# A gated short-convolution block: the input projection in triples of column groups, 20 block products each, in place of pairs with 7

## The chip, the cores and the metric

The kernel runs on one core of one Trainium2 chip. The metric is the device time of one execution in microseconds (us); lower is better. The engines are named as in the profile: PE (TensorE, the matmuls), PEld (its weight loads), DVE (VectorE), ACT (ScalarE), POOL (GpSimd) and SP (SyncE, which here only issues DMA transfers).

## The reference, cut to what matters

With DEPTH = 1 only the first kind of layer is computed. x is 1024 tokens by 1024 features, `w_in` is 1024 by 8192 and `w_out` 2048 by 1024, all in float32.

```python
def rms_norm(x, g):
    y = xf * lax.rsqrt(jnp.mean(xf * xf, axis=-1, keepdims=True) + EPS)
    return y * g

def short_conv_mixer(u, w_in, conv_w, w_out):
    z, bg, cg, v = jnp.split(u @ w_in.astype(u.dtype), 4, axis=-1)
    y = bg * causal_dwconv(cg * v, conv_w) * jax.nn.silu(z)
    return y @ w_out.astype(u.dtype)

h = h + rms_norm(short_conv_mixer(rms_norm(h, pre_norm), ...), post_norm)
```

The convolution has three taps over the tokens and works on each of the 2048 channels by itself. The four parts Z, BG, CG and V of the projection are 2048 columns each.

## The kernel before, in words

**Tiling.** The channels are cut into 16 chunks of 128. A group is one chunk of one part: 128 columns of `w_in`, so there are 64 groups. The projection's result stands transposed: the 128 channels of a group on the partitions, the tokens in two halves of 512, each in a PSUM bank (`bank`). Every operand of a product is split into a high and a low part in float32r, and every product of two blocks is three matmuls (low by high, high by low, high by high, L189 to L191), each with a 128x128 weight block and 512 tokens.

**Pairs and their 7 products.** `PAIRS` has 32 pairs of groups, (CG, V) and then (Z, BG) of each chunk. Pair 0 is multiplied plainly (`plain`, L384 to L386, 96 matmuls). Each of the other 31 is a 2x2 by 2x2 block product (two groups by two halves of the inner dimension, against two halves of the inner dimension by two halves of the tokens) done with 7 block products in place of 8; `ORDER` is "abcedfg". A block product has four 128-wide parts of the inner dimension and three matmuls each, so a pair has 84. Seven operand forms of the tokens (`u_a` to `u_g`, high and low) are built once, in the head, and stay in SBUF: `new_u`, L352 and L355 for those read straight from the transposed tokens in PSUM, L489, L531, L532, L545 and L547 for the others.

**What the other engines do for a pair.** POOL forms the four sums of weight blocks, each 128x512 (`add_s`, L133 to L137). `split_w` splits the weights in four parts: ACT makes the high part (L140), DVE the low part (L141). PSUM is read by ACT (`snap`, L197) and DVE (`after`, L213 to L236). POOL multiplies the gates (L220, L226, L228). When a chunk's CG and V are there, `conv` runs the three taps, one on ACT (L583) and two on DVE (L585), over all 1024 tokens. `y_done` stores the chunk's y to DRAM.

**The operands of the output projection.** The output projection is one 2x2 by 2x2 block product in 7 as well. Sums of blocks of y and of `w_out` are made in DRAM during the projection by accumulating DMAs on POOL's queue (`more`, L241; `add_y`, `fetch_t`, `add_t`). Then 28 units of 1 MB are fetched (`fetch_unit`), split (`split_unit`), and multiplied (`out_mm`, L718 to L720, 672 matmuls), with the post norm between and behind.

**What sets the order.** `tc.manual_schedule()`: each engine works through its instructions in the order in which the program issues them. An instruction that waits holds up all that stand behind it on its engine. So the order of the calls in the loop over pairs (products, `after`, `split_w` of the next pair, `add_s` of the next pair) is the order on every engine.

**The head.** Tokens are loaded, their norm is folded into the transposes on PE (L340), and the first token half is read out as operand forms a and b. Pair 0's products for that half and the first products of pair 1 (b, a) stand on PE between the transposes of the second token half and the building of the forms c to g.

Of the kernel before, what the change touches and what calls it, by code (L numbers as in the profile page):

```python
# [8 lines left out]
F32 = mybir.dt.float32  # L9
# [9 lines left out]
def kernel(  # L19
# [26 lines left out]
    KH = NK // 2  # L46
    TH = NT // 2
# [10 lines left out]
    up = ctx.enter_context(tc.tile_pool(name="up", bufs=7))  # L58
    wp = ctx.enter_context(tc.tile_pool(name="wp", bufs=3))
    raw = ctx.enter_context(tc.tile_pool(name="raw", bufs=3))  # L60
# [21 lines left out]

# [27 lines left out]
    PAIRS = [(c, tys) for c in range(NC) for tys in ((CG, V), (Z, BG))]  # L110
    raws, sums, wt = {}, {}, {}

    def fetch(p, rows=(0, 1)):
        if p >= len(PAIRS):
            return
        c, tys = PAIRS[p]
        if p not in raws:
            raws[p] = raw.tile([P, 2, NK, P], F32, tag="raw", name=f"raw_{p}")
        for n in rows:
            c0 = tys[n] * CI + c * P  # L120
            nc.sync.dma_start(raws[p][:, n], wiv[:, :, c0 : c0 + P])

    def add_s(p, part):

        if p >= len(PAIRS):
            return
        r = raws[p]
        a11, a12, a21, a22 = (flat(r[:, n, k * KH : (k + 1) * KH]) for n in (0, 1) for k in (0, 1))
        if part == 0:
            sums[p] = raw.tile([P, 4, HB], F32, tag="sum", name=f"sum_{p}", bufs=1)  # L130
        s = sums[p]
        if part == 0:
            nc.gpsimd.tensor_add(s[:, 1], a21, a22)  # L133
            nc.gpsimd.tensor_sub(s[:, 0], s[:, 1], a11)  # L134
        else:
            nc.gpsimd.tensor_sub(s[:, 2], a11, a21)  # L136
            nc.gpsimd.tensor_sub(s[:, 3], a12, s[:, 0])  # L137
# [5 lines left out]
    def split_w(p, part):  # L143

        if p >= len(PAIRS):
            return
        n = 2 * HB if part < 3 else HB
        tag = "w8" if part < 3 else "w4"
        if p == 1 and part == 1:
            t = raw.tile([P, 2, n], F32R, tag="raw", name=f"w{part}_{p}")  # L150
        else:
            t = wp.tile([P, 2, n], F32R, tag=tag, name=f"w{part}_{p}", bufs=3 if part < 3 else 2)
        if part == 0:
            src = flat(raws[p][:, 0])
        elif part == 3:
            src = flat(raws[p][:, 1, KH:])
        else:
            src = flat(sums[p][:, 2 * (part - 1) : 2 * part])
        split(src, t[:, 0], t[:, 1])
        wt[p, part] = t  # L160


    WHERE = {"a": (0, 0), "b": (0, HB), "c": (1, 0), "e": (1, HB), "d": (2, 0), "f": (2, HB), "g": (3, 0)}
    ORDER = "abcedfg"
    UH, UL = {}, {}

    def new_u(i):
        u = up.tile([P, 2, KH, HB], F32R, tag="u", name=f"u_{i}")
        UH[i], UL[i] = u[:, 0], u[:, 1]

    for i in ORDER[:-1]:
        new_u(i)

    banks = {}

    def product(p, i, ks=None):

        part, off = WHERE[i]
        w = wt[p, part]
        which = {"b": "y", "e": "v", "f": "v"}.get(i, "x")  # L180
        first = i in "abe"
        if first and (p, which) not in banks:
            banks[p, which] = bank(f"p{which}_{p}")
        ps = banks[p, which]
        for k in range(KH) if ks is None else ks:
# [9 lines left out]
    def snap(p, i):  # L195
        t = snp.tile([P, HB], F32, tag="sn", name=f"sn{i}_{p}", bufs=5)
        nc.scalar.copy(t, banks[p, "v" if i == "e" else "x"])  # L197
        sn[p, i] = t
# [5 lines left out]
    def after(p, i):  # L204
# [4 lines left out]
        if i in "ace":  # L209
            snap(p, i)  # L210
# [629 lines left out]
```

## Time and profile before

| what | value |
|---|---|
| median of 2 runs | 796.25 us (795.71 to 796.79) |
| the profiled execution, its own time | 797.52 us |
| the profiled execution, span in the trace | 795.7 us |
| PE busy, matmuls and transposes | 784.0 us, 3502 |
| DVE, POOL, ACT busy | 472.7, 337.0, 307.3 us |
| bytes moved by DMA | 116.49 MB |
| first matmul of pair 0 | 13.23 us |
| first matmul of the output projection | 636.53 us |
| last matmul | 788.63 us |

The profile is one execution; its time is 1.8 us longer than its span and 1.27 us over the median. The trace gives each instruction's start and length in us from the span's start. A matmul's own length is modelled, so the pace of PE is read from the distance between starts. A row of the grouped view names the line, engine, operation, output and inputs, the number of instructions, their busy time and mean length in ns, and then the idle time of the engine just ahead of them with what ended it. Some matmul records are missing from the trace.

### The profile page before, as it was taken

Reading aid. Unit: us, or ns where it says so; the run is one execution under the profiler, and the core shown is the slowest. Engines: PE = TensorE matmul, PEld = TensorE weight load, DVE = VectorE, ACT = ScalarE, POOL = GpSimd, SP = SyncE. Lnnn points to the kernel's source line nnn. Section 1 sums busy time; section 2 is a strip of 40 time slices with the busy share of each in tenths; the row PEclk is TensorE's granted clock in tenths of the full one; section 3 lists DMA queues with packets and bytes.
Section 4 is the critical chain, followed back from the end, with each engine's and each line's share of the span. In section 5 each row is a group of like instructions: output and inputs, shape, how many; then the busy total and the mean of one; then the engine's idle time right before and its main releaser. Section 6 shows DMA issues by size and latency. Waiting matters only on the chain.

```text
span 795.7 us, 9148 instructions
## 1 busy us (share of the span) xinstructions
PE 784.0 (99%) x3502; PEld 648.5 (82%) x3502; DVE 472.7 (59%) x518; ACT 307.3 (39%) x425; POOL 337.0 (42%) x256
## 2 busy tenths in 40 slices
PE   8999999999999999999999999999999999999996
PEld 8877888888888887888788888888888888888885
DVE  6799646554645454654466565656565856633766
ACT  7555333232333333333333343323233646544441
POOL 1608646465454555547664545455445110000020
PEclk9999999999999999999999999999999999999999
DMA  9131373829191928295633425161606589455237
GB/s 317 55 106 40 81 210 68 224 54 253 25 264 38 241 66 212 75 257 114 137 96 90 126 60 145 40 170 16 173 14 180 217 278 348 176 202 212 105 112 259
DMA packets 100811, 116.49 MB, mean 146 GB/s; under 512 B 4328, under 2 KB 69920, under 8 KB 98720
## 3 DMA queue, kind: packets, MB, share of 16 engines
q1 hardware_dynamic: 91536, 99.13, 37.6%
q0 software_dynamic: 9216, 16.78, 13.8%
q8 instruction: 27, 0.44, 0.2%
q14 instruction: 16, 0.13, 0.0%
q10 hardware_dynamic: 16, 0.00, 0.0%
HBM read 92.83 MB, written 44.04 MB: 172 GB/s over the span
## 4 chain that ended last, share of the span: by engine, by line
PE 90%; issue 4%; POOL 3%; DVE 1%; ACT 1%; DMA 0%; DVEq 0%; POOLq 0%; ACTq 0%
PE px L189 13%; PE px L191 13%; PE px L190 13%; PE pv L191 7%; PE pv L189 7%; PE pv L190 7%; PE po_x L718 4%; PE po_x L719 4%; PE po_x L720 4%; PE py L191 3%; PE py L189 3%; PE py L190 3%; PE po_v L718 2%; PE po_v L720 2%; PE po_v L719 2%
## 5 line engine op out<-in xcount | busy, mean ns | idle before, releaser
L141 DVE TENSOR_TENSOR w<-sum,w 128x1024 fp32r<-128x1024 f32 x62 | 88.2, 1422 | 120.3 <-ACT w L140 120.3
L141 DVE TENSOR_TENSOR w<-raw,w 128x1024 fp32r<-128x1024 f32 (+1 forms) x62 | 94.3, 1522 | 5.9 <-ACT w L140 5.9
L140 ACT CAST w<-sum 128x1024 fp32r<-128x1024 f32 x62 | 64.9, 1047 | 65.8 <-issue 54.5
L585 DVE SCALAR_TENSOR_TENSOR cv<-gpad,cw,cv 128x1024 f32<-128x1024 f32 x32 | 55.6, 1739 | 33.1 <-ACT cv L583 32.5
L140 ACT CAST w<-raw 128x1024 fp32r<-128x1024 f32 (+1 forms) x62 | 51.4, 831 | 50.0 <-PE py L191 41.4
L758 POOL TENSOR_TENSOR acc<-xr,acc 128x512 f32<-128x512 f32 x4 | 6.9, 1734 | 117.6 <-DVE acc L757 117.6
L136 POOL TENSOR_TENSOR sum<-raw 128x512 f32<-128x512 f32 x31 | 55.7, 1798 | 0.0
L134 POOL TENSOR_TENSOR sum<-sum,raw 128x512 f32<-128x512 f32 x31 | 54.0, 1743 | 2.4
L223 DVE TENSOR_TENSOR snc<-pv,snc 128x512 f32<-128x512 f32 x30 | 20.7, 690 | 54.8 <-PE pv L191 54.8
L220 POOL TENSOR_TENSOR sne<-sne,cv 128x512 f32<-128x512 f32 x15 | 20.8, 1387 | 70.7 <-DVE sne L218 70.7
L137 POOL TENSOR_TENSOR sum<-raw,sum 128x512 f32<-128x512 f32 x31 | 50.7, 1637 | 0.0
L133 POOL TENSOR_TENSOR sum<-raw 128x512 f32<-128x512 f32 x31 | 47.4, 1529 | 7.0 <-DVE w L141 7.0
L189 PE MATMUL px<-u_g,w 128*128 128x512 f32 x124 | 48.5, 391 | 1.4 <-DVE sne L218 0.8
L189 PE MATMUL px<-u_c,w 128*128 128x512 f32 x124 | 48.5, 391 | 1.3 <-ACT sna L197 1.3
L189 PE MATMUL px<-u_d,w 128*128 128x512 f32 x124 | 48.4, 390 | 0.2 <-ACT snc L197 0.2
L189 PE MATMUL py<-u_b,w 128*128 128x512 f32 x124 | 48.5, 391 | 0.0
L189 PE MATMUL px<-u_a,w 128*128 128x512 f32 x124 | 48.3, 390 | 0.0
L190 PE MATMUL px<-u_c,w 128*128 128x512 f32 x124 | 48.3, 389 | 0.0
L190 PE MATMUL px<-u_g,w 128*128 128x512 f32 x124 | 48.3, 389 | 0.0
L191 PE MATMUL px<-u_g,w 128*128 128x512 f32 x124 | 48.3, 389 | 0.0
L191 PE MATMUL px<-u_d,w 128*128 128x512 f32 x124 | 48.3, 389 | 0.0
L191 PE MATMUL py<-u_b,w 128*128 128x512 f32 x124 | 48.3, 389 | 0.0
(248 smaller groups left out, 2051.2 us busy)
## 6 DMA issues: line engine op xcount, KB each, us to landing
raw<-in_sc_w_in SPq DMA_DIRECT2D x64, 512.0 KB, 7.7
s_d<-cv SPq DMA_DIRECT2D x32, 256.0 KB, 2.2
t_d<-in_sc_w_out SPq DMA_DIRECT2D x32, 256.0 KB, 5.9
s_d<-cv POOLq DMA_DIRECT2D x16, 256.0 KB, 6.1
t_d<-in_sc_w_out POOLq DMA_DIRECT2D x16, 256.0 KB, 7.3
t_d<-t_d POOLq DMA_DIRECT2D x16, 256.0 KB, 4.3
y_d<-cv SPq DMA_DIRECT2D x8, 512.0 KB, 3.8
s_d<-s_d POOLq DMA_DIRECT2D x16, 256.0 KB, 6.1
```

Of the source, the lines that this page charges most:

```text
L134: nc.gpsimd.tensor_sub(s[:, 0], s[:, 1], a11)
L136: nc.gpsimd.tensor_sub(s[:, 2], a11, a21)
L137: nc.gpsimd.tensor_sub(s[:, 3], a12, s[:, 0])
L140: nc.scalar.copy(hi, src)
L141: nc.vector.tensor_sub(lo, src, hi.bitcast(F32))
L189: nc.tensor.matmul(ps, lo, UH[i][:, k], start=first and k == 0, stop=False, skip_group_check=True)
L190: nc.tensor.matmul(ps, hi, UL[i][:, k], start=False, stop=False, skip_group_check=True)
L191: nc.tensor.matmul(ps, hi, UH[i][:, k], start=False, stop=last, skip_group_check=True)
L585: nc.vector.scalar_tensor_tensor(cv, gpad[:, j : j + L], tap(c, j), cv, op0=ALU.mult, op1=ALU.add)
L718: nc.tensor.matmul(ps, lo, u[:, 0, k], start=first, stop=False, skip_group_check=True)
L719: nc.tensor.matmul(ps, hi, u[:, 1, k], start=False, stop=False, skip_group_check=True)
L720: nc.tensor.matmul(ps, hi, u[:, 0, k], start=False, stop=last, skip_group_check=True)
```

## The change

**Triples and 20 products.** The 64 groups stand in one list in the order CG, V, Z, BG of each chunk. The first four are multiplied plainly (192 matmuls). The other 60 are 20 triples. A triple is three groups by four quarters of the inner dimension, against four quarters by two token halves: 24 block products, done as 20. Each block product has two 128-wide parts and three matmuls each, so a triple has 120 matmuls. A triple no longer falls on a chunk's border: since a chunk has four groups, the parts in the triple's columns 1, 2, 0 (`COL`) run (CG, V, Z), (BG, CG, V), (Z, BG, CG), (V, Z, BG) and then start again. The text below and the prediction call these four kinds P0, P1, P2 and P3.

**Operand forms.** 18 forms of the tokens, each a high and a low part of 2x512 columns, are kept (`up`, 18 buffers). Eight are the blocks b00 to b31 themselves, read from PSUM. For the others the head adds and subtracts blocks (`make`, on DVE or POOL, L585, L587, L589) and splits the result (`finish`: ACT L126, DVE L127). The forms u_17, 6, 4, 11, 16, 10, 2 and 19 are finished behind the first splits of triple 0.

**Weights.** `sums` forms the weight sums of the next triple in place and in `e` (17 adds of 128x256 and one of 128x512 on POOL, L176 to L191). `split_w` splits units of two products' weights, A to J, into four buffers; six of the ten units are two pieces of 128x256.

**PSUM.** The 20 products run through five chains (`CHAINS`), each in one bank. Where a product is a sum that is needed more than once, `read` copies or adds the bank (ACT L313, L315; DVE L319, L321) and the next product of the chain adds on to the same bank. So that product can start only when the read is done.

**Gates and convolution.** `use` and `when` issue a gate or half of a convolution as soon as what it needs has been read; the convolution runs by halves of 512 tokens (ACT L267, DVE L269 twice per half).

**The rest.** Accumulating DMAs of y wait in a list (`later`), of which one is issued behind products 4 and 12 of each triple. The output projection's operands come in 56 units of 512 KB.

In the loop a step s is one product of `ORDER` and what is issued behind it:

```diff
-    ORDER = "abcedfg"
+    ORDER = (7, 9, 1, 8, 3, 5, 14, 17, 18, 6, 4, 11, 0, 15, 16, 10, 2, 13, 12, 19)
+    CHAINS = {"X": (1, 5, 18, 11, 10, 12, 19), "Y": (9, 3, 17, 4, 15, 16), "V": (7, 8, 14), "Z": (6, 2), "W": (0, 13)}
+    GROUPS = [(c, ty) for c in range(NC) for ty in (CG, V, Z, BG)]
+    TRIPLES = [GROUPS[n : n + 3] for n in range(4, len(GROUPS), 3)]
+    COL = (1, 2, 0)
...
+    LAST = {(1, 0): 14, (1, 1): 16, (2, 1): 10, (2, 0): 2, (0, 0): 13, (0, 1): 19}
...
+    def product(t, i):
+        ch, first = CHAIN[i]
+        if first:
+            banks[t, ch] = bank(f"p{ch}_{t}")
+        x, off = wf.pop((t, i))
+        for kk in range(2):
+            s = slice(off + kk * P, off + (kk + 1) * P)
+            pass3(banks[t, ch], x[:, 0, s], x[:, 1, s], U[i], kk, first and kk == 0, kk == 1)
...
+        elif ty == V:
+            when({(c, "cg", h)}, (c, "g", h), lambda: gate_g(c, h, src, sign, direct))
+            when({(c, "g", h)} | ({(c, "cv", 0)} if h else set()), (c, "cv", h), lambda: conv(c, h))
...
+    SUMS = {1: (0, 1), 2: (2,), 3: (3, 4), 5: (5,), 6: (6, 7), 8: (8, 9), 10: (10, 11), 18: (12, 13), 19: (14, 15)}
+    SPLIT = {3: "E", 6: "FG", 9: "H", 10: "I", 14: "J"}
+    NEXT = {14: "A", 18: "B", 19: "C", 20: "D"}
...
+        for s, i in enumerate(ORDER, 1):
+            product(t, i)
+            read(t, i)
+            if t == 0 and s < 4:
+                first_chunk(s - 1)
+            for unit in SPLIT.get(s, ""):
+                split_w(t, unit)
+            for unit in NEXT.get(s, ""):
+                split_w(t + 1, unit)
+            sums(t + 1, SUMS.get(s, ()))
```

The head, behind the last transposes and PE's plain products for the first two groups:

```diff
+    stage_tile()
+    make(dve, temp(7), "-", b21, b20)
+    finish(8)
+    finish(7)
...
+    make(dve, temp(2), "+", temp(11), b10)
+    make(dve, temp(2), "+", temp(2), b20)
+    head.close()
...
+    for n in (2, 3):
+        plain(n, 1, range(NK))
+    sums(0, range(12))
+    for unit in "ABCD":
+        split_w(0, unit)
+    sums(0, range(12, 16))
...
+    for i in (17, 6, 4, 11, 16, 10, 2, 19):
+        finish(i)
```

Now three places in the order. A trailing number in a name is the tile's running number, and "x2" is two such instructions in a row. The first is DVE in the head, in the kernel after, behind the first weight splits of triple 0: `s_` are staged forms, `u_` finished ones, `cv` and `gpad` the first chunk's convolution, `pY` the bank of chain Y.

```order
L127 TENSOR_TENSOR u_691<-s_417,u_691 128x512 x2
L127 TENSOR_TENSOR u_696<-s_417,u_696 128x512 x2
L127 TENSOR_TENSOR u_701<-s_535,u_701 128x512 x2
L127 TENSOR_TENSOR u_706<-s_535,u_706 128x512 x2
L127 TENSOR_TENSOR u_711<-s_569,u_711 128x512 x2
L127 TENSOR_TENSOR u_716<-s_569,u_716 128x512 x2
L127 TENSOR_TENSOR u_721<-s_570,u_721 128x512 x2
L127 TENSOR_TENSOR u_726<-s_571,u_726 128x512 x2
L269 SCALAR_TENSOR_TENSOR cv_751<-gpad_602,cw,cv_751 128x512 x2
L274 SCALAR_TENSOR_TENSOR gpad_602<-pp_1_489,gpad_602 128x512
L269 SCALAR_TENSOR_TENSOR cv_751<-gpad_602,cw,cv_751 128x512 x2
L321 TENSOR_TENSOR sn_0_0_744<-sn_0_0_744,pY_763 128x512
```

The 16 low halves of the eight late forms and the first chunk's convolution stand ahead of the first DVE read of triple 0 (L321), for which product 3 waits. Ahead of these rows stand 30 instructions of `make` and `finish` (L585 to L589 and L127, nearly all 128x512 from SBUF) and the first weight splits. Before, the forms c, d and g were made between products of pair 1:

```order
L532 TENSOR_TENSOR u_c<-xb,u_c 128x1024 x2
L545 TENSOR_TENSOR xa<-xb,xa 128x1024 x2
L141 TENSOR_TENSOR w_1_518<-sum_348,w_1_518 128x1024
L532 TENSOR_TENSOR u_d<-xa,u_d 128x1024 x2
L547 TENSOR_TENSOR xa<-xa,xb 128x1024 x2
L532 TENSOR_TENSOR u_g<-xa,u_g 128x1024
```

These were 9 instructions of 128x1024 and stood beside PE's products of pair 1; now 46 instructions, nearly all 128x512, stand behind PE's last transposes.

On ACT the same place in the kernel after shows the high halves of the eight late forms ahead of the reads of product 7 (`pV`, L315), for which product 8 waits:

```order
L126 CAST u_701<-s_535 128x512 x2
L126 CAST u_706<-s_535 128x512 x2
L126 CAST u_711<-s_569 128x512 x2
L126 CAST u_716<-s_569 128x512 x2
L126 CAST u_721<-s_570 128x512 x2
L126 CAST u_726<-s_571 128x512 x2
L315 ACTIVATE sn_0_0_744<-pV_737 128x512
L315 ACTIVATE sn_3_0_746<-pV_737 128x512
L290 ACTIVATE gpad_602<-pp_1_485 128x512
```

Before, no read of PSUM on ACT stood behind so many casts.

The second place is the border of triples 4 and 5 (kind P0 to P1) on DVE, after: the reads of products 10, 2 and 13, the convolution's four half-taps between them, and then the low part of unit B, which product 9 of the next triple needs.

```order
L319 TENSOR_TENSOR gpad_602<-pY_1691,gpad_602 128x512
L321 TENSOR_TENSOR sn_3_1_1787<-sn_3_1_1787,pX_1700 128x512
L319 TENSOR_TENSOR sn_3_0_1685<-pZ_1780,sn_3_0_1685 128x512
L269 SCALAR_TENSOR_TENSOR cv_1860<-gpad_602,cw,cv_1860 128x512 x4
L319 TENSOR_TENSOR sn_0_0_1683<-pW_1808,sn_0_0_1683 128x512
L127 TENSOR_TENSOR wB_1878<-e_1687,wB_1878 128x512
L127 TENSOR_TENSOR wC_1889<-raw_1_1611,wC_1889 128x512
```

The split of unit B stands behind the read of product 13, and that behind the convolution.

Before, the convolution of a chunk (two instructions of 128x1024) stood between splits like this, with the next pair's first split behind:

```order
L236 TENSOR_TENSOR gpad<-px_1922,sna_1935 128x512
L585 SCALAR_TENSOR_TENSOR cv_2045<-gpad,cw,cv_2045 128x1024 x2
L141 TENSOR_TENSOR w_13_2049<-raw_1813,w_13_2049 128x512
L213 TENSOR_TENSOR sna_2065<-py_2073,sna_2065 128x512
L141 TENSOR_TENSOR w_14_2087<-raw_1944,w_14_2087 128x1024
```

The next split there was the fourth part of a pair's weights; now it is the second unit of ten.

The third place is POOL in triple 7 (kind P3), after: the gate of the first token half (L276), which is due behind step 7, and what stands ahead of it, ten sums of triple 8 and one DMA issue.

```order
L176 TENSOR_TENSOR raw_3_2305<-raw_3_2305 128x256 x2
L177 TENSOR_TENSOR e_2377<-raw_3_2305,raw_0_2307 128x512
L178 TENSOR_TENSOR e_2377<-e_2377,raw_0_2307 128x256
L179 TENSOR_TENSOR raw_2_2303<-raw_3_2305,raw_2_2303 128x256
L180 TENSOR_TENSOR e_2377<-raw_2_2303 128x256
L327 DMA s_d<-s_d 128x512
L181 TENSOR_TENSOR raw_0_2307<-e_2377,raw_0_2307 128x256 x2
L182 TENSOR_TENSOR raw_0_2307<-raw_0_2307 128x256
L183 TENSOR_TENSOR e_2377<-raw_3_2305 128x256
L276 TENSOR_TENSOR gpad_602<-sn_3_0_2419,gpad_602 128x512
```

Four more sums of 128x256 (steps 18 and 19 of triple 6) stand just ahead of the first row.

Before, a gate of the same kind (L228) stood behind the second pair of sums of a pair and DMA issues:

```order
L136 TENSOR_TENSOR sum_1423<-raw_1299 128x512
L137 TENSOR_TENSOR sum_1423<-raw_1299,sum_1423 128x512
L241 DMA t_d<-in_sc_w_out 128x512 x2
L241 DMA t_d<-t_d 128x512
L228 TENSOR_TENSOR gpad<-snc_1464,sne_1479 128x512
L241 DMA t_d<-t_d 128x512
```

What moved there: the gate had four sums of 128x512 per pair around it; it now has up to ten instructions of the next triple ahead of it within one triple.

More of the change, by code (lines that the diff above doesn't have):

```diff
@@ L307 @@
         load_x(t)
[L308 removed]
+    wg = {}
     warm = small.tile([P, 1], F32, tag="sd1", name="warm")
@@ L800 @@
             out_mm(i, h, q)
-        for _ in "uy":
+        for _ in range(4):
             split_unit()
```

775 lines of the change are left out of this document (388 added, 387 removed).

## The prediction, as recorded before the run

> **What bounds the kernel now.** I read the page's busy shares, its 40 slices and the chain that ended last, then PE's waits, then windows.
>
> ```profile
> PE 784.0 (99%) x3502; PEld 648.5 (82%) x3502; DVE 472.7 (59%) x518; ACT 307.3 (39%) x425; POOL 337.0 (42%) x256
> PEclk9999999999999999999999999999999999999999
> PE 90%; issue 4%; POOL 3%; DVE 1%; ACT 1%; DMA 0%; DVEq 0%; POOLq 0%; ACTq 0%
> PE px L189 <- ACT sna L197: 1.3, 2, 0.7
> 80.00:600.00 520.00, 518.71 (x2287) 428.82 (x2286) 290.52 (x260) 175.61 (x233) 279.97 (x212) 1.00 0.51 124
> 780.00:796.00 16.00, 9.02 (x40) 7.13 (x38) 9.44 (x26) 1.97 (x6) 0.00 (x0) 0.91 0.68 243
> ```
>
> PE is busy 784.0 of 795.7 us at full clock, and 90% of the last chain is PE. The longest of its wait rows is 1.3 us in all. From 80 to 600 us it is busy 518.71 of 520, DVE 290.52 (56%) and POOL 279.97 (54%). So only the number of matmuls times their pace matters, as long as the others deliver in time. The pace is read from starts, since a matmul's own 0.39 overlaps the next:
>
> ```profile
> 61.74 0.39 PE L189 MATMUL px<-u_a,w 128*128 128x512 f32 x1
> ...
> 299.60 0.39 PE L190 MATMUL px<-u_c,w 128*128 128x512 f32 x1
> ...
> 300.51 0.39 PE L191 MATMUL pv<-u_e,w 128*128 128x512 f32 x1
> ...
> 636.53 0.39 PE L718 MATMUL po_x<-ou_a,oy_a 128*128 128x512 f32 x1
> ```
>
> Four matmuls in 0.91 us give 0.227; over 96 of the output projection (21.74 us) it is 0.2264, which I use. At 61.74 us pair 2 begins: 96 + 84 = 180 of the 2700 projection matmuls are done. From the output projection's first matmul, 636.53, to the end of the span are 159.2 us.
>
> **The gain.** 192 plain and 20 x 120 matmuls are 2592, 108 fewer: 108 x 0.2264 = 24.5 us. The pace itself should stay: same form, 128x128 weights, 512 tokens. Were nothing else to change, the span would be 771.2.
>
> **The head.** The forms cost DVE and ACT work, and PE's cover for it is 96 plain matmuls. The rows:
>
> ```profile
> 13.23 0.50 PE L384 MATMUL pp<-u_a,wn 128*128 128x512 f32 x1
> 26.42 0.19 PEld L386 LDWEIGHTS pp<-u_b,wn 128*128 128x128 f32 x1
> 26.64 0.39 PE L386 MATMUL pp<-u_b,wn 128*128 128x512 f32 x1
> L489 DVE TENSOR_TENSOR u_e<-xb,u_e x4: 684/788/1508, 32.5 to 43.7; 128x512 fp32r<-128x512 f32 x4
> 40.00:50.00 10.00, 10.00 (x48) 8.35 (x47) 9.90 (x12) 6.13 (x7) 1.08 (x1) 1.00 0.36 105
> 50.00:60.00 10.00, 9.33 (x42) 7.44 (x41) 8.83 (x10) 5.18 (x8) 0.06 (x1) 1.00 0.37 106
> L140 ACT CAST w<-raw 128x512 fp32r<-128x512 f32 x31 | 18.9, 608 | 0.0
> 27.06 1.29 POOL L133 TENSOR_TENSOR sum<-raw 128x512 f32<-128x512 f32 x1
> L136 POOL TENSOR_TENSOR sum<-raw 128x512 f32<-128x512 f32 x31 | 55.7, 1798 | 0.0
> ```
>
> Columns of a window: stretch and length, then busy time and number for PE, PEld, DVE, ACT and POOL, clock and DMA. DVE is already busy 9.90 and 8.83 of 10 us there. The first 48 plain matmuls end near 26.9, as before. The next 48 (10.9 us) and the transposes between them bring the last transposed block to about 44 us; two reads and four rebuilds on ACT, six at 0.61 or a little more, let the first sum of blocks start at about 48. Behind it DVE has 30 instructions of 128x512: 0.68 clean to 0.94 (the mean of L489's four) beside POOL. I take 0.73, nearest to the clean end since POOL makes only five sums: 22 us, so the last `make` ends at 70 (68 to 75). PE's other 96 plain matmuls end at 44 + 21.7 = 65.9.
>
> Then three waits follow one another.
> - POOL's first sums of triple 0 stand behind the last `make`, whose space they use. Up to product 7's weights: four 128x256 and one 128x512 sum, then cast and low half, about 6.5 us: product 7 starts at 76.5, PE idle 10.6. The trace has no 128x256; half of 1.29 to 1.80 bounds it at 0.65 to 0.90 if nothing is fixed.
> - Product 8 goes on in product 7's bank and needs ACT's copies of it. They stand behind 16 casts of late forms, each 0.61 and paced by DVE's low halves at 0.68 to 0.79: 16 x 0.73 = 11.7 us, beginning about when product 7 does, after the units' casts. Products 9 and 1 hide 2.7. Product 8 starts near 92, idle about 11.5.
> - Product 3 needs DVE's read of product 9, behind the same low halves and the first chunk's four half-taps (0.75 each) and a gate: it starts near 98.5, idle about 4.5. Four more products, and step 9 starts at 103.7 (97 to 110).
>
> By then 192 + 48 = 240 of 2592 matmuls are done, and 2352 x 0.2264 = 532.5 us are left. The old kernel is at (103.7 - 61.74) / 0.2264 + 180 = 365 at that time, so the head alone costs 125 x 0.2264 = 28.3 us, more than the gain. Without any later stall: 103.7 + 532.5 + 159.2 = 795.4.
>
> The Trainium skill, "TensorE: Matmul & The Clock Gate", Part 1, says that PE, after an idle window of about 3.4 us, runs at half clock until about 3.4 us of work have passed. The trace of before has no such gap; its only row under full clock is the last one above, 0.91, where PE works 9.02 of 16 us. By that rule each of the three gaps would cost up to 1.7 us; the first two bursts (4.1 and 1.4 us of work) end in another wait that hides most of it, so the sum would be about 2 us longer.
>
> **The steady state.** A triple is 120 x 0.2264 = 27.2 us, a product 1.36. Products must now wait for reads and for splits at ten places, and a single late read stops PE. Prices:
>
> ```profile
> L218 DVE TENSOR_TENSOR sne<-px,sne 128x512 f32<-128x512 f32 x30 | 20.5, 685 | 0.0
> L228 POOL TENSOR_TENSOR gpad<-snc,sne 128x512 f32<-128x512 f32 x15 | 22.0, 1468 | 8.1 <-DVE snc L223 8.1
> L583 ACT ACTIVATE cv<-gpad,cw 128x1024 f32<-128x1024 f32 x16 | 18.5, 1156 | 52.0 <-POOL gpad L228 32.6 <-DVE gpad L236 19.4
> L585 DVE SCALAR_TENSOR_TENSOR cv<-gpad,cw,cv 128x1024 f32<-128x1024 f32 x32 | 55.6, 1739 | 33.1 <-ACT cv L583 32.5
> L225 ACT ACTIVATE snc<-snc 128x512 f32<-128x512 f32 x15 | 9.5, 632 | 68.1 <-DVE snc L223 68.1
> L241 POOL DMA_DIRECT2D t_d<-t_d x16: 812/836/844, 121.2 to 374.2; - x16
> L241 POOL DMA_DIRECT2D t_d<-in_sc_w_out x16: 810/968/1126, 113.7 to 365.5; - x16
> POOL s_d L241 <- DMA s_d<-s_d: 53.9, 8, 7.6
> raw<-in_sc_w_in SPq DMA_DIRECT2D x64, 512.0 KB, 7.7
> t_d<-in_sc_w_out POOLq DMA_DIRECT2D x16, 256.0 KB, 7.3
> t_d<-t_d POOLq DMA_DIRECT2D x16, 256.0 KB, 4.3
> ```
>
> Half of L585's row is 0.87 per half-tap, half of L583's 0.58.
>
> P0's border. Product 2 (step 17) ends. DVE reads it 0.69, POOL's gate 1.47, ACT's first tap 0.6, four half-taps 2.6 to 3.5, the read of product 13 behind them 0.69, Silu 0.63, the cast of unit B 0.6 and its low half 0.7: 8.0 to 8.9 us, and 0.35 for the last matmul's tail and the weight load (0.39 less 0.2264, and 0.19). Product 9 of the next triple is due four products later, 5.43. The stall is 2.9 to 3.8; I take 3.2.
>
> P1's border. The same chain with two half-taps, behind step 18: 0.69 + 1.47 + 0.6 + 1.3 to 1.7 + 0.7 + 0.35 = 5.1 to 5.5, due in 4.08: 1.2.
>
> P2. Product 8 waits for ACT's reads of product 7, which stand behind a tap that waits for DVE's gate: 0.5 to 1.8, I take 1.3.
>
> P3. The gate due behind step 7 stands on POOL behind 13 sums of 128x256, one of 128x512 and DMA issues. From the two DMA issues of step 17 on, POOL has 2 x 0.97 + 13 x 0.65 to 0.90 + 1.8 + 0.84 = 13.0 to 16.3 us of work, and ten products are 13.6: a backlog of 0 to 3. Gate, tap, two half-taps and the read of product 17 take 1.47 + 0.6 + 1.7 + 0.69 + 0.35 = 4.8, due 4.08 later: 0.7 to 4. The next triple's weights add to it: three fetches of 512 KB are issued at step 15, six products (8.2 us) ahead of POOL's first sum of them, and two at a time now take 7.7; three may be 0 to 4 us late. I take 3.4. Two later places (product 12 behind a half-tap, unit B once more) give 1.1 and 0.75.
>
> One period of four triples: 3.2 + 1.2 + 1.3 + 5.25 = 10.9 us, 6 to 13 by the ends. There are five periods, the first partly inside the head's waits; 4.5 x 10.9 = 49 us (27 to 59).
>
> **What costs nothing.** The late fetches cost PE nothing outside P3 as long as POOL has 2 to 4 us of a triple left; without that cover each triple would lose what they are late. The output operands carry the same bytes and splits in twice the units, beside 159 us of PE. The stores of y and the accumulating DMAs, some six of which are left when the loop ends, at 4.3 to 7.3 us each, are done before the units that read them, 54 us into the output projection.
>
> **The sum.** 103.7 + 532.5 + 49 + 159.2 = 844.4 us span; 1.8 outside: 846. The profiled execution stands 1.27 over its median, so 845 against 796.25.
>
> **Rivals.**
> - Steady waits are covered, the head as forecast. Against it stands that each border's chain is longer than its slack by rows alone; for it, that after one stall the others have caught up, that half a row may be too dear an estimate, and that 128x512 forms run at 0.68 where POOL is idle. 795 to 808 us, within 2%.
> - Full gain: faster. The point is the ACT and DVE queue in the head: only if product 7's and 9's reads came out by about 80 us, that is if the 16 late splits took no time ahead of them, and if the steady waits were under 4 us, would it end under 780. The gain alone gives 771 + 1.8 = 773. Rows of L140 and L489 speak against it.
> - POOL becomes the bound. Per triple: 17 x 0.77 to 0.90, one 1.8, three to four gates and products at 1.4, three DMA issues at 0.84 to 0.97: 23 to 25 of 27.2 us. It has 2 to 4 us left, and if a DMA issue waited 6 us for its input, as eight do now (53.9 us, up to 7.6), the triple would take 30 us or so: 795 + 20 x 3.5 = 865, up to 890. Against it stands that the new order leaves eight to ten products, 11 to 14 us, between one DMA and the next that reads it, where 4.3 to 7.3 are needed. The late fetches speak for it.
>
> [...]
>
> **How the numbers follow.** About 2% (16 us) is what a measurement of this kernel tells from no change. The forecast, head loss and steady stalls, has 0.72 and its own range is 815 to 865. Stalls covered: 0.12, 795 to 808. POOL the bound: 0.13, 865 to 890. Full gain: 0.03. So faster 0.03, same 0.12, slower 0.85. The range that leaves out two in ten reaches from 808, above the covered case, to 873, into POOL's.
>
> **What would show it.** In the head: PE idle of about 10, 11 and 4.5 us between 65 and 99 us, ended by DVE `w` L127 (unit A), ACT `sn` L315 and DVE `sn` L321; step 9 of triple 0 at 97 to 110. In the middle: PE busy about 92% in place of 99.8%, with waits for DVE `w` L127 at every border of a P0 and P1, and for DVE L321 in P3. PE's pace between waits at 0.2264. POOL busy 75 to 90%. The output projection should begin near 685 and end 159 later. I am wrong if PE's waits in the middle are under 15 us in all, if products 8 and 3 of triple 0 start before 85, or if the matmuls' pace is not 0.2264.

## The result and the profile after

The changed kernel takes 953.61 us (952.51 to 954.71) against 796.25: a ratio of 1.1976 with a 95% interval of 1.1907 to 1.2045. It is slower, as forecast, but by 157 us and not by 49; the forecast range ended at 873.

The page of the profile after, parts 1, 2 and 4, in the rows shown of before:

```profile
PE 812.2 (85%) x3394; PEld 649.1 (68%) x3394; DVE 649.2 (68%) x890; ACT 346.9 (36%) x681; POOL 464.0 (49%) x514
PEclk9896589998999998999999989989999999999999
PE 45%; DVE 27%; POOL 10%; issue 8%; ACT 6%; DMA 4%; SPq 1%; DVEq 0%; POOLq 0%; ACTq 0%
```

Three things stand in these rows. The last chain is now PE for 45% and DVE for 27%, where it was 90% PE. PE is busy for longer than before although it has 108 matmuls fewer: the clock row is no longer full. And DVE's busy time rose by 176.5 us.

PE's waits in the kernel after (what waited, for what; us in all, times, longest):

```profile
PE pY L130 <- DVE sn L321: 41.3, 15, 5.8
PE pY L130 <- DVE wB L127: 25.7, 15, 3.5
PE pY L130 <- DVE gpad L321: 19.2, 12, 3.3
PE pV L130 <- ACT sn L315: 16.6, 6, 14.0
PE pV L130 <- DVE wA L127: 11.7, 1, 11.7
PE pp L130 <- DVE wn L467: 7.0, 3, 5.8
```

With the smaller rows that is 134 us, against 4.8 before. Chain Y's waits for DVE (product 4 and others, and product 9 for wB) are 86 of them.

Busy time by stretch in the kernel after, first the head, then the loop (columns as in the prediction; the clock stands ahead of the DMA share):

```profile
60.00:144.00 84.00, 50.60 (x187) 39.59 (x186) 64.91 (x81) 27.47 (x53) 45.31 (x47) 0.74 0.12 38
144.00:780.00 636.00, 551.36 (x2262) 436.70 (x2261) 448.45 (x602) 210.15 (x461) 384.33 (x437) 0.95 0.43 105
```

PE is idle 33 of 84 us in the head and 85 of 636 in the loop, and what it does in the head it does at a mean clock of 0.74. The mean clock of the whole run is 0.940 of full.

Three starts place the stages (the forecast's in brackets): product 7 at 86.0 us (76.5), step 9 of triple 0 at 127.00 (103.7), the output projection's first matmul at 785.0. So of the 108.4 us by which the span of 952.8 exceeds the forecast 844.4, the head has 23.3, the loop 76.5 (658.0 from step 9 on against 532.5 + 49), and the output projection 8.6 (167.8 against 159.2): there PE now waits 6.0 us for two splits (3.4 and 2.6), with half clock behind the longer wait.

### The profile page after: what moved, and what is told of

Its sections match the earlier page's. It is cut to its first block, busy times and chain, and to the rows that moved or that the text cites. A ratio compares the mean times of both kernels' runs of the same rounds, so it can differ in the third digit from the quotient of the medians.

```text
span 952.8 us, 9998 instructions
## 1 busy us (share of the span) xinstructions
PE 812.2 (85%) x3394; PEld 649.1 (68%) x3394; DVE 649.2 (68%) x890; ACT 346.9 (36%) x681; POOL 464.0 (49%) x514
## 4 chain that ended last, share of the span: by engine, by line
PE 45%; DVE 27%; POOL 10%; issue 8%; ACT 6%; DMA 4%; SPq 1%; DVEq 0%; POOLq 0%; ACTq 0%
PE pY L130 6%; PE pY L132 5%; PE pY L131 5%; DVE cv L269 4%; DVE sn L319 3%; PE pX L130 3%; DVE wG L127 3%; PE pX L131 3%; PE pX L132 3%; DMA raw<-in_sc_w_in 3%; POOL gpad L276 2%; PE po_x L764 2%; PE po_x L762 2%; PE po_x L763 2%; DVE u L127 2%
## 5 line engine op out<-in xcount | busy, mean ns | idle before, releaser
L276 POOL TENSOR_TENSOR gpad<-sn,gpad 128x512 f32<-128x512 f32 x25 | 27.3, 1092 | 155.1 <-DVE sn L319 117.6
L269 DVE SCALAR_TENSOR_TENSOR cv<-gpad,cw,cv 128x512 f32<-128x512 f32 x64 | 59.2, 931 | 46.8 <-ACT cv L267 45.7
L298 POOL TENSOR_TENSOR cv<-cv,sn 128x512 f32<-128x512 f32 x31 | 39.8, 1291 | 70.6 <-ACT sn L297 70.6
L267 ACT ACTIVATE cv<-gpad,cw 128x512 f32<-128x512 f32 x32 | 22.6, 722 | 115.5 <-POOL gpad L276 101.4
L126 ACT CAST wJ<-raw 128x256 fp32r<-128x256 f32 x20 | 8.1, 407 | 112.0 <-PE pW L132 88.6
L130 PE MATMUL pY<-u,wB 128*128 128x512 f32 x40 | 19.6, 489 | 25.7 <-DVE wB L127 25.7
L321 DVE TENSOR_TENSOR sn<-sn,pX 128x512 f32<-128x512 f32 x45 | 30.6, 680 | 14.9 <-PE pX L132 14.9
L127 DVE TENSOR_TENSOR wG<-e,wG 128x512 fp32r<-128x512 f32 x20 | 38.2, 1910 | 0.0
L321 DVE TENSOR_TENSOR sn<-sn,pY 128x512 f32<-128x512 f32 x45 | 30.5, 679 | 9.7 <-PE pY L132 9.6
L127 DVE TENSOR_TENSOR wD<-raw,wD 128x256 fp32r<-128x256 f32 x40 | 32.4, 848 | 5.7 <-ACT wD L126 5.7
L127 DVE TENSOR_TENSOR wF<-e,wF 128x256 fp32r<-128x256 f32 x20 | 35.7, 1785 | 0.0
L176 POOL TENSOR_TENSOR raw<-raw 128x256 f32<-128x256 f32 x40 | 35.2, 900 | 0.0
L181 POOL TENSOR_TENSOR raw<-e,raw 128x256 f32<-128x256 f32 x40 | 33.9, 975 | 0.3
L130 PEld LDWEIGHTS pY<-u,wB 128*128 128x128 f32 x40 | 8.5, 212 | 33.7 <-DVE wB L127 28.2
L327 POOL DMA_DIRECT2D s_d<-s_d x24 | 19.7, 820 | 23.3 <-DMA s_d<-s_d 11.8
```

What stands on the lines that cost most here:

```text
L127: nc.vector.tensor_sub(lo, src, hi.bitcast(F32))
L130: nc.tensor.matmul(ps, lo, u[:, 0, kk], start=first, stop=False, skip_group_check=True)
L176: 0: lambda: (add(w2[:, 0], w2[:, 0], w2[:, 1]), add(w2[:, 2], w2[:, 1], w2[:, 2])),
L181: 5: lambda: (sub(w0[:, 2], e[:, 3], w0[:, 2]), sub(w0[:, 0], e[:, 3], w0[:, 0])),
L269: nc.vector.scalar_tensor_tensor(cv, g[:, j : j + HB], tap(c, j), cv, op0=ALU.mult, op1=ALU.add)
L276: nc.gpsimd.tensor_mul(g, src, g)
```

## The experiments

Each kernel is the changed one with one edit unless said otherwise, and each time is that of one execution; the two of the changed kernel lie 2.2 us apart. The kernel before took 795.71 to 797.24 us beside them.

**1. Fill PE's gaps (e1_fill).** Discarded matmuls go into a bank that the next product overwrites, ahead of the products that wait longest.

```diff
+    def fill(ps, n):
+        b = B[0, 0]
+        for _ in range(n):
+            nc.tensor.matmul(ps, b[:, 0, 0, :P], b[:, 0, 0], start=True, stop=True, skip_group_check=True)
+    HEAD = {1: 48, 2: 12, 4: 70, 5: 24}
+    STEADY = {(1, 2): 13, (3, 11): 23, (0, 11): 7}
...
+        fill(banks[t, "W"], HEAD.get(s, 0) if t == 0 else STEADY.get((t % 4, s), 0))
```

> This kernel adds matmuls whose results are thrown away, at the places where PE waits longest in the changed kernel: 22 ahead of the third plain group, 48, 12, 70 and 24 ahead of products 7, 9, 8 and 3 of the first triple, and per period of four triples 13 ahead of product 9 (P1), 23 and 7 ahead of product 4 (P3, P0). Theory (an idle PE falls to half clock, and the work behind the gap pays): PE has 60 us more work and the kernel gets faster all the same, to about 920 us (905 to 932); PE's clock row is full in the loop, time at half clock falls from 117 us to under 25. Rival (the clock is granted by something other than PE's idle time, or the half clock is hidden in other waits): no faster than 948 us, clock row as before.

Measured: 925.33 us, 28.3 less, with 384 matmuls more. The mean clock is 0.995, the time at half clock falls from 115 to 9 us by the trace's clock records, and the clock row of its page is full:

```profile
PEclk9999999999999999999999999999999999999999
```

What the half clock looks like in the kernel after, behind the 5.8 us wait of product 4 in a P3 triple (start, length):

```profile
359.40 0.39 PE L132 MATMUL pZ<-u,wE 128*128 128x512 f32 x1
365.61 0.80 PE L130 MATMUL pY<-u,wF 128*128 128x512 f32 x1 [5.82 <-DVE sn L321]
366.20 0.63 PE L131 MATMUL pY<-u,wF 128*128 128x512 f32 x1
366.62 0.63 PE L132 MATMUL pY<-u,wF 128*128 128x512 f32 x1
```

Behind the wait the starts are 0.42 us apart and more, not 0.2264. What waits of different length leave behind them is seen in four stretches of 2 us of the same kernel, behind waits of 2.04, 5.82, 3.28 and 2.56 us in this order:

```profile
266.30:268.30 2.00, 2.00 (x10) 1.63 (x9) 2.00 (x4) 0.00 (x0) 1.41 (x2) 1.00 0.00 0
365.80:367.80 2.00, 2.00 (x5) 1.63 (x6) 1.62 (x4) 0.00 (x0) 0.00 (x0) 0.50 0.03 8
568.40:570.40 2.00, 2.00 (x5) 1.61 (x6) 1.65 (x4) 0.00 (x0) 2.00 (x3) 0.50 0.75 270
798.80:800.80 2.00, 1.93 (x8) 1.27 (x8) 1.43 (x2) 0.00 (x0) 0.83 (x1) 1.00 0.37 131
```

The granted clock is 0.50 behind the two longer ones and full behind the others. In this kernel every wait of 3.08 us and more that began at full clock has half clock at its end or within 0.5 us behind it. Length alone does not decide below that: one wait of 2.29 us has it too, though the one of 2.56 has not.

```profile
768.41 0.50 PE L130 MATMUL pY<-u,wF 128*128 128x512 f32 x1 [2.29 <-DVE sn L321]
769.60:773.00 3.40, 3.40 (x10) 2.65 (x9) 1.39 (x4) 0.00 (x0) 0.00 (x0) 0.50 0.00 0
```

In other runs a wait of 3.46 us leaves the clock full (run 2, at 402.4 us) and one of 2.03 does not (run 5, at 381.8). So idle time of PE costs twice, once as a wait and mostly once more behind it when it comes near 3 us; adding work that is thrown away gives the second part back. The rule of the Trainium skill ("TensorE: Matmul & The Clock Gate", Part 1) that the prediction weighed, half clock after an idle window of about 3.4 us, agrees with the trace on the long waits; the waits of 2.29 and 3.08 us are shorter than its figure, and that of 3.46 in run 2 is not. The prediction's "about 2 us" was for the three gaps of the head; the gaps filled here, in the head and in the loop, gave 28.3.

**2. Move the DMA issue (e2_dma).**

```diff
-            if s in (4, 12) and len(later) > 0 and t > 0:
+            if s in (12, 13) and len(later) > 0 and t > 0:
```

> The accumulating DMAs of y that POOL issues behind product 4 of each triple are issued behind product 13 instead, the rest is the same. Theory (a DVE operation that runs when POOL issues a DMA and goes on with sums is held until that burst of sums is over): DVE's wF and wG splits from e, now 1785 and 1910 ns in the mean with single ones of 3.2 to 3.95 us, fall under 1300 ns each with none over 2 us; product 4's waits (60 us in all for chain Y's L130) fall by half; 900 to 918 us. Rival (POOL's sums alone hold DVE and the DMA issue only stands beside them): both means stay over 1600 ns and the time within 8 us of 953.

Measured: 919.74 us, 33.9 less. What it takes away is seen in the kernel after, DVE and POOL of a P0 triple, with the DMA issue:

```profile
260.54 0.83 POOL L327 DMA_DIRECT2D s_d<-s_d  x1
260.80 3.94 DVE L127 TENSOR_TENSOR wG<-e,wG 128x512 fp32r<-128x512 f32 x1
261.11 1.71 POOL L181 TENSOR_TENSOR raw<-e,raw 128x256 f32<-128x256 f32 x2
262.51 0.99 POOL L182 TENSOR_TENSOR raw<-raw 128x256 f32<-128x256 f32 x1
263.21 0.98 POOL L183 TENSOR_TENSOR e<-raw 128x256 f32<-128x256 f32 x1
264.26 1.07 POOL L184 TENSOR_TENSOR e<-e,raw 128x256 f32<-128x256 f32 x1
```

and in the next triple, which issues no DMA there:

```profile
295.21 1.94 POOL L181 TENSOR_TENSOR raw<-e,raw 128x256 f32<-128x256 f32 x2
295.34 1.22 DVE L127 TENSOR_TENSOR wG<-e,wG 128x512 fp32r<-128x512 f32 x1
```

The same split takes 3.94 us with the issue just ahead of it and 1.22 without. It ends 0.55 us behind the fourth of POOL's sums in a row, which ends at 264.19; these start 0.70 us apart, each before the one ahead has ended. In the two kernels, the splits wF from e and wG (min/median/max in ns), first after, then with the DMA moved:

```profile
L127 DVE TENSOR_TENSOR wF<-e,wF x20: 415/851/3309, 125.0 to 762.3; 128x256 fp32r<-128x256 f32 x20
L127 DVE TENSOR_TENSOR wG<-e,wG x20: 676/951/4109, 126.7 to 763.0; 128x512 fp32r<-128x512 f32 x20
```

```profile
L127 DVE TENSOR_TENSOR wF<-e,wF x20: 415/563/949, 125.2 to 729.8; 128x256 fp32r<-128x256 f32 x20
L127 DVE TENSOR_TENSOR wG<-e,wG x20: 684/1221/1225, 126.9 to 730.4; 128x512 fp32r<-128x512 f32 x20
```

None of these over 1.23 us is left. The waits of product 4 in P0 and P1 go with them, but for one of 0.4; that in P3 falls from 5.8 to 4.2 us in most triples. Behind the DMA issue of t_d, which was not moved, a few DVE operations of 1.95 to 1.98 us stay. The theory holds on durations; the time was 2 us outside its band.

**3. Leave POOL's sums out (e5_nosums).** For t > 0 `sums` returns at once, and the splits read raw weights.

> POOL's weight sums are left out for all triples but the first (the splits take raw weights in their place, so the output is not the reference's); the gates, the DMA issues behind product 4 and all of DVE's and ACT's work stay. Theory (what DVE loses, it loses to POOL's sums): DVE's 128x256 splits fall to 0.42 us each and wF and wG from e to 0.42 and 0.68, even where a DMA is issued; product 4's waits fall under 10 us in all, the wait for wB (25.7 us) stays, and the time is about 885 us (870 to 905). Rival (the DMA issue alone holds DVE): single wF and wG of over 2 us stay, and over 930 us.

Measured: 883.35 us, 70.3 less. DVE's splits are all clean now, although the DMA behind product 4 is still issued:

```profile
L127 DVE TENSOR_TENSOR wF<-raw,wF x39: 415/418/420, 122.7 to 693.8; 128x256 fp32r<-128x256 f32 x39
L127 DVE TENSOR_TENSOR wG<-raw,wG x19: 685/686/687, 156.9 to 694.1; 128x512 fp32r<-128x512 f32 x19
```

So the DMA issue alone holds nothing: it takes the issue and a burst of sums behind it. With run 2 this leaves the sums as the larger cause and the DMA issue as what makes it worse; why the issue does so is not shown by any run. The 70.3 us are the price of the sums as a whole: the run takes POOL's work away together with its hold on DVE, and no run parts the two. Product 4's wait in P3 falls to 1.4 us, product 3's in P2 (1.5) goes. Not every DVE operation is slowed. In the kernel after, the reads that take one operand from PSUM (min/median/max) stand in the same stretches and are never long:

```profile
L321 DVE TENSOR_TENSOR sn<-sn,pY x45: 669/675/690, 118.1 to 770.4; 128x512 f32<-128x512 f32 x45
```

The Trainium skill ("SBUF — State Buffer", "Who interferes with whom") has it that a DVE instruction contends with POOL when it has two inputs from SBUF or runs in a two-port mode, and that whichever comes second is blocked for the whole of the other's instruction. The trace agrees for these operations, 0.69 us at most with one input from PSUM and up to 4.11 with two from SBUF; but the long ones last over four of POOL's instructions, not one.

**4. Split unit B earlier (e3_b).**

```diff
-    ORDER = (... 0, 15, 16, 10, 2, 13, 12, 19)
+    ORDER = (... 0, 15, 16, 13, 10, 2, 12, 19)
-    NEXT = {14: "A", 18: "B", 19: "C", 20: "D"}
+    NEXT = {14: "A", 16: "B", 19: "C", 20: "D"}
```

> Product 13 goes ahead of products 10 and 2, so that unit B's buffer is free two products earlier, and unit B is split behind step 16, ahead of the convolution. Theory (the border waits come from B's split standing behind the convolution): PE's waits for wB, 25.7 us now, fall under 6 us, and with the half clock behind them 915 to 928 us. Rival (DVE is the limit at the border, the wait only moves to product 8 or 3 of the next triple): wB's wait goes and others grow by as much, over 943 us.

Measured: 943.06 us, 10.5 less. The wait for wB fell from 25.7 to 3.4 us, but others grew by as much: PE's idle time as a whole went only from 140.6 to 139.4 us. What was gained is the clock, whose mean rose from 0.940 to 0.955, since fewer of the waits are long. Three rows of its waits:

```profile
PE pV L130 <- ACT sn L315: 24.3, 6, 14.7
PE pX L130 <- DVE sn L321: 13.7, 10, 2.6
PE pV L130 <- DVE wC L127: 10.7, 4, 2.7
```

They were 16.6, 4.4 and none. The rival was right, by both of its marks: with the convolution where it is, the next split and the next reads are waited for in B's place.

**5. Convolve later (e6_defer).** Each half of a convolution goes into a list and is issued two steps later, behind that step's reads and splits.

```diff
-            when(..., (c, "cv", h), lambda: conv(c, h))
+            when(..., (c, "cvq", h), lambda: held_back.append((step[0] + 2, c, h)))
...
+            convs(step[0])
             sums(t + 1, SUMS.get(s, ()))
```

> Each half of the convolution is issued two steps later than what it needs, behind that step's reads and splits; nothing else moves. Theory (the border waits and P3's wait come from reads and splits that stand behind a convolution which itself waits for POOL's gate): the waits for wB fall under 3 us, product 4's wait in P3 (5.8 us) under 1.5, product 3's in P2 (1.5) under 0.5; those of product 4 in P0 and P1 (2.0 and up to 3.3) stay, since DVE is held there by POOL; with the half clock that goes with the long ones 870 us (855 to 895). Rival (DVE's work as a whole is the limit, and the waits only move): over 925 us.

Measured: 913.99 us, 39.6 less, half of what was expected and between the two bands. The wait for wB is 6.8 us, but the half-taps, two steps later, run into POOL's next burst and hold other reads: chain X's wait for sn rose from 4.4 to 14.5 us.

**6. Hold the rebuilds (e7_hold).** One copy of a column on POOL, which waits for the scaled second half, stands ahead of `rebuild` in the head.

```diff
+    hold = small.tile([P, 1], F32, tag="hold", name="hold", bufs=1)
+    nc.gpsimd.tensor_copy(hold, xs[NT - 1][:, :1])
     for k in (4, 5, 0, 1, 6, 7, 2, 3):
         rebuild(k, 0)
```

> In the head POOL's eight rebuilds of the first token half wait until DVE and ACT have scaled the second half, by a copy of one column on POOL, as the kernel before had it. Theory (DVE's five small operations, 1.06 to 1.21 us each in place of 0.16, and the scaling, 3.4 us in place of 1.5, are stretched by the rebuilds, and PE's 5.8 us wait for the third plain weights comes from that): that wait falls under 2 us and the time to 942 to 949 us. Rival (the forms' chain on DVE starts no earlier for it, because the rebuilds are then late): within 2 us of 953.

Measured: 947.73 us, 5.9 less. DVE in the kernel after, and then with the hold:

```profile
23.69 1.13 DVE L99 TENSOR_SCALAR hr_pre<-r_pre 128x4 f32<-128x4 f32 x1
27.34 3.40 DVE L530 TENSOR_SCALAR xb<-xb,rs_pre 128x1024 f32<-128x1024 f32 x2
```

```profile
22.28 0.17 DVE L99 TENSOR_SCALAR hr_pre<-r_pre 128x4 f32<-128x4 f32 x1
22.94 1.42 DVE L530 TENSOR_SCALAR xb<-xb,rs_pre 128x1024 f32<-128x1024 f32 x2
```

An operation on 128x4 elements takes 1.13 us beside POOL's rebuilds and 0.17 without. It has one tensor input, so two inputs from SBUF are not the only case that is slowed. The theory's band was met (947.73, in 942 to 949), and product 7 starts at 79.6 us in place of 86.0.

**7. Finish the late forms behind step 2 (e4_late).** `finish` of the eight late forms moves into the loop, behind the reads of products 7 and 9.

> The eight late operand forms are finished behind step 2 of the first triple instead of ahead of step 1, so that the reads of products 7 and 9 stand ahead of them on ACT and DVE. Theory (products 8 and 3 wait 14.0 and 4.3 us for reads that stand behind the late forms): those two waits fall under 3 us together, a wait of a few us for u_17 or u_6 comes, triple 1 starts near 122 us in place of 143.3, and the time is 928 to 938 us. Rival (the forms are the limit wherever they stand: products 17, 18, 6 wait as long as 8 and 3 did): triple 1 starts after 138 us and the time is over 947 us.

Measured: 959.24 us, 5.6 more; triple 1 starts at 146.41 us. Product 8 waits 2.2 us in place of 14.0, but the next read on ACT now stands behind the casts:

```profile
PE pX L130 <- ACT gpad L313: 8.8, 1, 8.8
```

The rival is right: the work is the limit, not its place.

**8 and 9. Leave forms out (e9_nolate, e10_noforms).** In e9 `finish` of the eight late forms is left out, in e10 every `make` and `finish`; the products use another tile.

> The eight late operand forms are not finished: their products use another form's tile (the output is not the reference's). Theory (products 8 and 3 of the first triple wait 18 us because DVE and ACT have 16 casts and 16 low halves to do at that time, wherever they stand): those waits fall under 5 us together, triple 1 starts at 121 us (118 to 126) in place of 143.3, and 930 us (924 to 936). Rival (the reads are late for another reason, the first chunk's convolution or the raw weights of triple 1): triple 1 starts after 132 us and over 940 us.

> None of the 13 made operand forms is built (neither sums of blocks nor splits; their products use block b00, so the output is not the reference's). It prices the forms. Theory (the head's loss is the forms' work on DVE, ACT and POOL): product 7 starts near 74 us in place of 86, triple 1 near 106 (102 to 112) in place of 143.3, and 915 us (908 to 922). Rival (the head is late because of the first triple's weight sums and the half clock): triple 1 starts after 122 us and over 930 us.

Measured: 941.46 and 916.89 us; triple 1 starts at 130.53 and 105.19. The 13 forms cost 36.7 us together, as the theory of e10 had it. For e9 neither side was right: product 8's wait goes to 1.6 us, but product 3 now waits 6.0 for its read behind the first chunk's convolution.

**10. Together (e8_combo, e11_best, e13_apart, e14_fill).** e8 has the later convolution, the held rebuilds, all accumulating DMAs behind steps 11 to 15, and the sums of steps 5 and 6 behind step 7. e11 sets two DMAs further apart and fills the head; e13 is e8 with the second y DMA of a triple taken from another chunk; e14 is e13 with the head filled.

> Together: the later convolution halves, the held rebuilds, all accumulating DMAs issued behind products 11 to 15 of a triple, and in each triple the sums of step 5 and 6 behind step 7, so that P3's gate stands ahead of them. Theory (these are the causes in the loop, and they add): 835 us (815 to 860), with the loop's period of four triples near 113 us in place of 133, the rest of the loss in the head. Rival (each only uncovers the next): over 875 us.

> The combination of e8 with two of its DMAs set further apart (behind products 12 and 15 of the order, so that the second does not wait on POOL for the first), and with discarded matmuls in the head's gaps (4, 48, 13, 66 and 16). Theory (POOL waiting for a DMA makes the wait for wB of 6.3 us in the second half of the loop, and the head's half clock costs some 6 us): 855 us (845 to 866), period 115 us throughout. Rival (the second half is slow for another reason): over 870 us. Neither is below the kernel before.

> As e8, but of the two y DMAs that a triple issues behind products 12 and 13 of the order the second is one of another chunk, whose input was written in an earlier triple. Theory (in e8's second half POOL stands still for the landing of the first, 7.05 us in the one that was looked at, and the gates behind it are late): no POOL wait of over 3 us for an s_d DMA in the loop, the wait for wB under 5 us in all behind the first triple's 3.4, the period 116 us in the second half too, and 862 us (855 to 870). Rival (e11 was no faster for another reason, such as DVE's hold): second half still over 122 us a period, and over 872 us.

> The same with discarded matmuls in the head's gaps only (4, 48, 13, 66 and 16). Theory (the head's half clock costs 5 to 8 us beyond what its waits hide): 5 to 8 us less than the run without them, about 856 us. Rival (the head is bound by DVE to its end): within 2 us of it.

Measured: 878.79, 897.57, 863.95 and 857.45 us. e8 is 74.8 below the changed kernel, in the rival's band: its largest part, the later convolution, had been expected at some 84 us alone and gave 39.6. The parts measured alone give 39.6 + 33.9 + 5.9 = 79.4; the new place of the sums and of the t_d issues has no run of its own. In its second half POOL stood still for the first of two DMAs of one chunk before it could issue the second:

```profile
457.74 0.80 POOL L338 DMA_DIRECT2D s_d<-s_d  x1 [7.05 <-DMA s_d<-y_d]
```

e11 lost: its t_d issues now wait 2.8 to 6.1 us ahead of the border's gates, and the wait for wB rose from 14.8 to 20.6 us. e13 landed 2 us from what was expected: in its loop no s_d issue waits over 3 us any more, and the waits that are left (up to 7.6) stand behind the loop. The fill of the head gives 6.5 more, as forecast. None is near the kernel before.

**11. PE's program with little else (e12_bare).** e8 without the 13 forms and without the sums of all triples but the first.

> As e8, and the 13 made forms and the sums of all triples but the first are left out (the output is not the reference's). PE's program is that of the changed kernel. Theory (the saving of 108 matmuls is there, and all the rest is waiting for DVE, ACT and POOL): triple 1 starts near 98 us, the period is 110 to 113 us, and 792 us (782 to 805), against 772 of PE's matmuls alone. Rival (PE itself is slower with twice as many short products and bank changes): the pace between waits is over 0.229 us and the time over 815 us.

Measured: 804.03 us. The loop of it:

```profile
110.00:600.00 490.00, 482.00 (x2100) 392.34 (x2099) 316.46 (x558) 194.10 (x424) 103.97 (x101) 1.00 0.52 127
400.04 0.39 PE L132 MATMUL pW<-b,wG 128*128 128x512 f32 x1
401.85 0.39 PE L131 MATMUL pY<-b,wH 128*128 128x512 f32 x1
```

Eight matmuls in 1.81 us are 0.226 each, over a change of banks: the pace is that of before, and PE is busy 98% of the loop. The rival (a slower PE) is out, and the time is within the theory's 782 to 805. So the 24.5 us are saved on PE, and even with forms and sums free they are used up: the output projection begins at 635.4 us, 1.2 earlier than before, and itself takes 6.3 longer.

## Why the prediction was wrong

Two steps failed: the clock was left out of the sum, and DVE's operations beside POOL were priced too low, in the head and in the loop. None of the three signs by which the prediction said it would be wrong came up.

- **The gain** was right: 108 matmuls at an unchanged pace of 0.226 (run 11).
- **The signs and places of the waits** were right in the main. Product 7 waits for wA (11.67 us, forecast 10.6), 8 for ACT's reads (14.00, 11.5), 3 for DVE's (4.29, 4.5); the border of P0 waits 3.46 us for wB (3.2 forecast), that of P1 0.81 (1.2); product 12 in P3 0.87 (1.1). Product 9's 3.44 us for wB in the head was not on the list, and the 0.75 for unit B behind P3 did not come.
- **The clock** is the first step that failed. The prediction gave the rule one paragraph with 2 us and left it out of the sum, because "the trace of before has no such gap". But the prediction itself put gaps of 10.6, 11.5 and 4.5 us into the head and 3.2 and 3.4 into every period. In the kernel after, waits like these have half clock behind them; filling the gaps is worth 28.3 us (run 1).
- **P3's price** (3.4) is the term of the loop that was most mis-sized, and its mechanism was another: the wait is 5.8 us. The prediction had the gate late on POOL, behind the sums and late fetches. In the kernel after, POOL stands idle for 1.91 us ahead of that gate, because the read that it needs (L319) stands on DVE behind a split that is held:

```profile
355.06 3.31 DVE L127 TENSOR_TENSOR wF<-e,wF 128x256 fp32r<-128x256 f32 x1
359.23 0.68 DVE L319 TENSOR_TENSOR sn<-pV,sn 128x512 f32<-128x512 f32 x1
359.99 1.09 POOL L276 TENSOR_TENSOR gpad<-sn,gpad 128x512 f32<-128x512 f32 x1 [1.91 <-DVE sn L319]
361.87 3.08 DVE L269 SCALAR_TENSOR_TENSOR cv<-gpad,cw,cv 128x512 f32<-128x512 f32 x2 [1.96 <-ACT cv L267]
364.88 0.68 DVE L321 TENSOR_TENSOR sn<-sn,pY 128x512 f32<-128x512 f32 x1
```

- **DVE beside POOL** is the second step. "Product 8 in P2" (1.3) measured 0.5, while places that were not on the list came up: product 4 in P0 (2.0) and, in three of five, in P1 (3.1 to 3.3), product 3 in P2 (1.5). POOL's sums are behind them: run 2 takes product 4's away, run 3 product 3's too. The prediction took DVE's operations at 0.68 to 0.94 "beside POOL" and the two half-taps at 1.7. In fact a 128x256 split takes up to 3.3 us until POOL's burst is over (runs 2 and 3), and the two half-taps above take 3.08. The sums cost 70.3 us in all, and none of that stood in the sum as such: POOL was looked at as a queue that might be late, and not as an engine that slows DVE.
- **One period** of four triples took 133.0 us (249.65 to 382.66) against 108.7 of matmuls, so 24.3 were lost where the sum had 10.9. Without the sums (run 3) it took 119.5, so 10.8 were lost. That this meets the forecast is luck in part, since it holds half clock and has 1.4 us at P3's wait for product 4 in place of 3.4.
- **The head** was put at 28.3 us and cost 51.7: at 127.00 us the kernel before has done (127.00 - 61.74) / 0.2264 + 180 = 468 matmuls, 228 more. Measured alone, the forms are 36.7 of it (run 9) and the rebuilds 5.9 (run 6); filling the head's gaps gave 6.5 in run 10, and the rest has no run of its own. DVE's chain of forms, its first and last rows in the kernel after, began at 55.9 and not at 48, and took 28.2 us and not 22, with four of POOL's five sums of forms beside it:

```profile
55.91 1.28 DVE L587 TENSOR_TENSOR s<-xb,xa 128x512 f32<-128x512 f32 x2
...
81.59 2.48 DVE L585 TENSOR_TENSOR s<-s,xa 128x512 f32<-128x512 f32 x4
```

That product 7's wait comes near 10.6 us is luck: PE's plain products ended at 74.3 and not at 65.9, and product 7 started 1.9 us behind the last `make` and not 6.5, since the sum that it needs, one of POOL's first two, was done at 80.5.

- **The output projection**, put under "what costs nothing", took 8.6 us more, of which 6.0 are the waits for two splits.
- **Rivals**: POOL as the bound came nearest in size, and for another reason than its own: POOL is busy 60% of the loop (384 of 636 us), some 20 us a triple where the prediction had 23 to 25, and it is POOL that waits for DVE ahead of its gates:

```profile
POOL gpad L276 <- DVE sn L319: 117.6, 20, 12.9
```

In the loop the account is this: of the 125.5 us over 532.5 PE's idle time is some 85. The half clock is some 24, an estimate from the trace's clock records, which have PE working at 0.50 for 49 us there. The other 16 or so are not placed.

## What to carry to other kernels

When a change makes products smaller and lets them wait on each other's reads, price each wait twice: its length, and the slow clock behind it once it comes near 3 us. Price a DVE operation on two SBUF operands by what POOL does at that time and not by its size; put POOL's DMA issues where no burst of POOL work follows. A saving of 3% on the busiest engine is gone when the new waits and the slow clock behind them come to 3% of the time, so count the places that can wait before counting matmuls.

## What the runs showed of the hardware that was not expected

- A DVE subtraction of 128x512 that starts while POOL issues a DMA with four sums queued behind it takes 3.94 us; beside the same sums without the issue 1.22; alone 0.69. A 128x256 one: 3.3, 0.42 to 0.95, 0.42.
- 384 matmuls that compute nothing make this kernel 28.3 us faster.
- Four of DVE's six operations on 128x4 elements take 1.06 to 1.21 us beside POOL's rebuilds, the other two 0.15 and 0.17; without the rebuilds all six take 0.15 to 0.18. What is added does not shrink with the size.
- A sum of 128x256 on POOL takes 0.72 to 0.74 us where DVE is idle, and its lines have means of 0.77 to 1.10. Half of the 128x512 rows (0.65 to 0.90) was a fair bound for the first and too low for some of the second.
